# Chained PSUM sums for the gate and up projections, and the norm's second product moved to the gate's side

## The chip, the cores and the metric

The kernel runs on one core of a Trainium2 chip. The metric is the device time of one execution in microseconds (us). TensorE is called PE in the profile (PEld is its weight load), VectorE DVE, ScalarE ACT, GpSimd POOL, SyncE SP; a q behind an engine's name means its sequencer.

## What is computed

The reference is one step of a streaming encoder with one layer: attention with two groups of heads, an output projection with a residual, then a SwiGLU feed-forward block with a residual, and a last norm. There are 16 meta tokens, 512 of a prompt and 64 of a sample; the 576 of prompt and sample go through the feed-forward block. The change touches only the second half of a layer:

```python
x = x + mix @ lp['w_out']
h = rmsnorm(x, lp['norm_ffn_g'])
x = x + (jax.nn.silu(h @ lp['ffn_w_gate']) * (h @ lp['ffn_w_up'])) @ lp['ffn_w_down']
```

D_MODEL is 2048 and D_FF 5632; everything is float32.

## The kernel before

**Precision.** A float32 product is made of three matmuls. Each operand is split into a high part (rounded to the matmul's type, written by ACT, L156) and a low part (the difference, written by DVE, L153), and high x high, high x low and low x high are added in PSUM. Weights are split when they have been loaded: the tiles `wh` and `wl`, two buffers each. The tokens' operands are split once for a stage: `bh` and `bl`.

**Seven products for eight.** Gate, up and down multiply two by two blocks of 128 x 128 weights with two by two blocks of 128 x 288 tokens by Winograd's form of Strassen's scheme. `winograd` (L993) runs the seven products. Products 1, 2 and 4 take a block of the raw weights (a11, a12, a22) as it is; 5 and 7 take a sum and a difference that POOL makes (`subtotal`, L1013, called by `lhs`); 6 is made by DVE from 5's, and 3 by DVE from 6's. The sums lie in `ws`, three buffers. For each product, the matmuls with `wh` run over all slots (L1051: `bh` and `bl`), then those with `wl` (L1055). Then `take` adds the product to what the call makes, and `step` runs a piece of other work that is threaded in.

**Order and banks.** `ORDER` (L937) is 1, 2, 4, 5, 6, 3, 7, each product in a PSUM bank of its own. The down projection gives `chain=CHAIN` instead (L1263): 1, 5, 6, 2, 7, 3, 4, in three banks. Products 1, 6, 7 and 4 share bank "a", 5 and 3 bank "b", and 2 has "c". What lies in a shared bank is a running sum, which `take` reads at points on the way; a matmul into a shared bank has to wait until the last reading of it is done.

**Gate and up.** The loop over u (L1185, 22 times) makes 256 columns of gate, then of up: one `winograd` call each, with eight slots of 256 rows of the model dimension, so 7 x 24 matmuls. A call loads two raw tiles of 1 MB, one for each half of the slots (L1193). There are three buffers for them, one in pool `rw` and two in `fr`, so that one half of the next call can be loaded a call ahead, and the other goes where the first half of the present call lay. The result goes to a tile `c` of two rows f of 576 tokens, as four quarters c11, c12 (row 0) and c21, c22 (row 1): one buffer for the gate (tag `cg`), two for up (`cu`). `combined` (L1118) makes the take: an ACT copy of product 1 into a tile `s` (L1125) and seven DVE sums (L1128 to L1137). For c11 that is L1137, after product 2, the second of the call.

**After a pair of calls** (L1214): for each row f, DVE multiplies g by the token norm `rb2` (L1215), ACT takes the Silu (L1216), POOL multiplies w (up's result) by `rb2` (L1217) and by g (L1218), and the row is stored to DRAM. For u below 20, POOL then makes four sums of w's quarters (L1224 to L1227) in a view `t` of the gate's tile, and SP stores them (`sumspill`). Only when that store has read them may the next gate call write its tile.

**Down.** The results are brought back as operands by `builder` (L1141), in blocks of 4 slots or, for the last block, 2. Its first block is built during the last up call, by product in `ORDER` (L1153, `by_product`).

**What sets the order.** In these stages a scheduler that builds the program lays out each engine's instructions by when it expects them to be ready; the text's order is the priority. Only down's builder pins some. Loads and stores are issued by SP.

Of the kernel before, what the change touches and what calls it, by code (L numbers as in the profile page):

```python
# [13 lines left out]
AF = mybir.ActivationFunctionType  # L14
ALU = mybir.AluOpType
# [100 lines left out]
def encoder_step(  # L116
# [8 lines left out]
    V, S, G = nc.vector, nc.scalar, nc.gpsimd  # L125
# [10 lines left out]
    def load(dst, src):  # L136
        nc.sync.dma_start(dst, src)
# [11 lines left out]
    def f32(ap):  # L149
        return ap.bitcast(F32)  # L150
# [44 lines left out]
    def project(ps, wsrc, xs, dup=False):  # L195
        for hf in range(2):
            wh, wl = weights(
                wsrc[hf * 8 * P:(hf + 1) * 8 * P, :].rearrange("(k p) c -> p k c", p=P), 8, P, dup)
            for k in range(8):
                kc = hf * 8 + k  # L200
                mm3([ps[:, 0, 0:TH], ps[:, 1, 0:TH]], wh[:, k, :], wl[:, k, :],
                    halves(xs[kc][0]), halves(xs[kc][1]), kc == 0, kc == KC - 1)
                yield 0
# [110 lines left out]
    with ExitStack() as ph:  # L314
# [30 lines left out]
        with tc.tile_pool(name="xn", bufs=1) as xn:  # L345
# [59 lines left out]
            first = project(ps0, w_in[:, 0:P], xs1)  # L405
# [24 lines left out]
        for j, (o, n) in enumerate(tok):  # L430
            b = o // TH
# [194 lines left out]
    with ExitStack() as ph:  # L626
# [288 lines left out]
        first = st.spawn(0, latents())  # L915
# [12 lines left out]
    def pool(name, side="left"):  # L928
        cm = tc.tile_pool(name=name, bufs=1, side=side)
        return cm.__enter__(), lambda: cm.__exit__(None, None, None)  # L930
# [3 lines left out]
    rb2 = rw.tile([P, TQ], F32, name="rb2")  # L934
    sq2 = rw.tile([P, TQ], F32, name="sq2")
    operands = {}
    ORDER = (1, 2, 4, 5, 6, 3, 7)  # L937

    def pin(ins):
        if pinned[0]:  # L940
            tc.keep_in_program_order(ins)
# [3 lines left out]
    def operand(m, p, src):  # L945
        hi = bc.tile([P, QH], F32R, name=f"bh{p}_{m}")
        lo = bc.tile([P, QH], F32R, name=f"bl{p}_{m}")
        pin(S.activation(hi, src, AF.Copy))
        pin(V.tensor_tensor(lo, src, f32(hi), op=ALU.subtract))
        operands[m, p] = (hi, lo)  # L950

    def quarters(b1, b2):
        return b1[:, 0:QH], b1[:, QH:TQ], b2[:, 0:QH], b2[:, QH:TQ]

    def token_operands(pool, m, b1, b2):

        b11, b12, b21, b22 = quarters(b1, b2)

        def sum_tile():
            return pool.tile([P, QH], F32, name="bs", tag="bs", bufs=2)  # L960

        operand(m, 1, b11)
        yield
        operand(m, 2, b21)
        yield
        t = sum_tile()
        pin(G.tensor_tensor(t, b12, b11, op=ALU.subtract))
        operand(m, 5, t)
        yield
        pin(G.tensor_tensor(t, b22, t, op=ALU.subtract))  # L970
        operand(m, 6, t)
        yield
        pin(G.tensor_tensor(t, t, b21, op=ALU.subtract))
        operand(m, 4, t)
        yield
        operand(m, 3, b22)
        yield
        t = sum_tile()
        pin(G.tensor_tensor(t, b22, b12, op=ALU.subtract))
        operand(m, 7, t)  # L980
        yield

    def load_raw(pool, src, r0, nk, c0, bufs, tag="raw"):
        r = pool.tile([P, nk, 256], F32, name="raw", tag=tag, bufs=bufs)
        load(r, src[r0:r0 + nk * P, c0:c0 + 256].rearrange("(k p) c -> p k c", p=P))
        return r
# [121 lines left out]
    fw, close_fw = pool("fw")  # L1108
# [3 lines left out]
    fb, close_fb = pool("fb", "right")  # L1112


    def stile():
        return fr.tile([P, QH], F32, name="s", tag="s", bufs=4)

    def combined(c11, c12, c21, c22):  # L1118

        s = {}  # L1120

        def take(p, banks):
            if p == 1:
                s[1] = stile()
                S.activation(s[1], banks[1], AF.Copy)  # L1125
            elif p == 6:
                s[2] = stile()
                V.tensor_tensor(s[2], s[1], banks[6], op=ALU.add)  # L1128
                V.tensor_tensor(c12, s[2], banks[5], op=ALU.add)
            elif p == 3:  # L1130
                V.tensor_tensor(c12, c12, banks[3], op=ALU.add)
            elif p == 7:
                V.tensor_tensor(s[2], s[2], banks[7], op=ALU.add)
                V.tensor_tensor(c22, s[2], banks[5], op=ALU.add)
                V.tensor_tensor(c21, s[2], banks[4], op=ALU.subtract)
            elif p == 2:
                V.tensor_tensor(c11, s[1], banks[2], op=ALU.add)  # L1137

        return take

    def builder(m0, count, plain, ahead, by_product=False):  # L1141

        srcs = {}
        for m in range(m0, m0 + count):
            quarter = [actspill[2 * m + f, :, c] for f in range(2) for c in (slice(0, QH), slice(QH, TQ))]
            if plain:
                for p, src in zip((1, 2, 4, 5), quarter):
                    srcs[m, p] = src
            else:
                for p, src in zip(ORDER, (quarter[0], quarter[2], sumspill[m, :, 2], sumspill[m, :, 0],  # L1150
                                          sumspill[m, :, 1], quarter[3], sumspill[m, :, 3])):
                    srcs[m, p] = src
        todo = sorted(srcs, key=lambda mp: ORDER.index(mp[1])) if by_product else list(srcs)  # L1153

        def fetch(n):
            for m, p in todo[n:n + 1]:
                hi = bc.tile([P, QH], F32R, name=f"bh{p}_{m % 8}")
                lo = bc.tile([P, QH], F32R, name=f"bl{p}_{m % 8}")
                load(f32(lo), srcs[m, p])
                operands[m % 8, p] = (hi, lo)  # L1160

        for n in range(ahead):
            fetch(n)
        for n, (m, p) in enumerate(todo):
            fetch(n + ahead)
            hi, lo = operands[m % 8, p]
            pin(S.activation(hi, f32(lo), AF.Copy))
            yield
            pin(V.tensor_tensor(lo, f32(lo), f32(hi), op=ALU.subtract))
            yield  # L1170

    def token_norm():
# [4 lines left out]
        rsqrt(rb2, sq2)  # L1177
        yield

    blocks = [4, 4, 4, 4, 4, 2]  # L1180

    turn = 0
# [2 lines left out]
    for u in range(FC // 2):  # L1185
        out = {}
        for which, wsrc in (("g", w_gate), ("u", w_up)):
            first = turn == 0
            raws = []
            for hf in range(2):  # L1190
                if turn:
                    rp, bufs = (rw, 1) if turn % 3 == 0 else (fr, 2)
                    raws.append(load_raw(rp, wsrc, hf * 1024, 8, u * 256, bufs))  # L1193
                turn += 1
            c = fb.tile([P, 2, TQ], F32, name="c", tag="cg" if which == "g" else "cu", bufs=1 if which == "g" else 2)
            take = combined(*quarters(c[:, 0, :], c[:, 1, :]))
            done = [0]

            def step():
                if u == 0 and which == "u":  # L1200
                    next(norm, None)
                if u == FC // 2 - 1 and which == "u":
                    done[0] += 1
                    if done[0] > 2:
                        for _ in range(2 * blocks[0]):
                            next(start, None)

            if first:
                winograd(fw, fb, raws, range(4, 8), take, banks0, step=step)
            else:  # L1210
                winograd(fw, fb, raws, range(8), take, step=step)
            out[which] = c
        g, w = out["g"], out["u"]
        for f in range(2):  # L1214
            V.tensor_tensor(g[:, f, :], g[:, f, :], rb2, op=ALU.mult)  # L1215
            S.activation(g[:, f, :], g[:, f, :], AF.Silu)  # L1216
            G.tensor_tensor(w[:, f, :], w[:, f, :], rb2, op=ALU.mult)  # L1217
            G.tensor_tensor(w[:, f, :], w[:, f, :], g[:, f, :], op=ALU.mult)  # L1218
            if u < FC // 2 - 1:
                store(actspill[2 * u + f], w[:, f, :])  # L1220
        if u < FC // 2 - blocks[-1]:
            b11, b12, b21, b22 = quarters(w[:, 0, :], w[:, 1, :])
            t = g.rearrange("p f (h c) -> p (f h) c", h=2)
            G.tensor_tensor(t[:, 0, :], b12, b11, op=ALU.subtract)  # L1224
            G.tensor_tensor(t[:, 1, :], b22, t[:, 0, :], op=ALU.subtract)
            G.tensor_tensor(t[:, 2, :], b21, t[:, 1, :], op=ALU.subtract)
            G.tensor_tensor(t[:, 3, :], b22, b12, op=ALU.subtract)  # L1227
            store(sumspill[u], t)
# [12 lines left out]
    def plain_rows(m0, n, d, hs, slots, done):  # L1241
# [13 lines left out]
        for f in range(2):  # L1255
            for h in hs:
                c = y[2 * d + f][:, h * QH:(h + 1) * QH]
                V.tensor_tensor(c, c, banks[f, h], op=ALU.add)  # L1258
                done(2 * d + f, h)

    CHAIN = ((1, "a"), (5, "b"), (6, "a"), (2, "c"), (7, "a"), (3, "b"), (4, "a"))  # L1263

    def down_rows(m0, n, d, slots, step):
        raws = [load_raw(fr, w_down, m0 * 256, 2 * n, d * 256, 2)]
# [6 lines left out]

        winograd(yp, yp, raws, slots, take, step=step, chain=CHAIN)

# [42 lines left out]
    first = 0  # L1318
# [100 lines left out]
```

## Time and profile before

| | before |
|---|---|
| median of 3 runs | 2583.15 us (2583.13 to 2589.03) |
| the profiled execution | 2593.06 us |
| its span, first to last instruction | 2590.9 us |
| mean granted TensorE clock | 0.983 |
| gate and up, about | 1000 to 2010 us |
| of it 20 blocks u, 1054.5 to 1963.5 | 909 us |

The profile is of one execution. Its rows give the start, the length, the engine, the line and the operation with out<-in, and in brackets the idle time of that engine just before and what ended it. A matmul's row is some 0.29 us long, but a new one starts every 0.13 us. In a view of waits the columns are the total, the number and the longest. In a view of stretches each engine has its busy time and number of instructions, and behind them stand the granted TensorE clock, the busy share of the DMA engines and GB/s.

### The profile page before, as it was taken

What the parts mean: (1) busy time and instruction counts of PE and PEld (TensorE: products, weight loads), DVE (VectorE), ACT (ScalarE), POOL (GpSimd) and SP (SyncE); (2) the same over time, 40 slices, a digit from 0 to 9 for tenths busy, and PEclk for the clock granted to TensorE, in tenths of its full rate; (3) what the DMA queues carried; (4) which work ended last, traced back from release to release, by engine and by line L of the source; (5) the groups of instructions that cost most, each with busy time, mean ns of one, the idle gap of its engine ahead of it and who ended that gap; (6) DMA issues with size and microseconds to landing.
All of it is one profiled execution on the core that took longest, in us unless ns stands there. A gap on an engine that the chain in (4) does not pass through costs nothing. (4 is left out here: it accounts for less than half of the span.)

```text
span 2590.9 us, 44881 instructions
## 1 busy us (share of the span) xinstructions
PE 2464.9 (95%) x17847; PEld 2399.3 (93%) x17847; DVE 1837.4 (71%) x2955; ACT 1056.5 (41%) x1879; POOL 763.5 (29%) x614
## 2 busy tenths in 40 slices
PE   6999999989999999999999999999999899999997
PEld 5999999988999888999999999999999899999996
DVE  5455555556565568777677787777778899899874
ACT  5234333334443444333333333333334344444444
POOL 0000000000000265545545455464543221221244
PEclk9999999999999899999999999999999899999998
DMA  6433233334331553333333333333335543443334
GB/s 197 126 93 93 80 86 86 81 104 121 99 99 58 170 152 124 106 113 121 130 116 108 111 122 128 116 128 108 109 126 177 189 146 98 146 146 101 98 107 130
DMA packets 330563, 307.73 MB, mean 119 GB/s; under 512 B 24707, under 2 KB 298506, under 8 KB 330354
## 3 DMA queue, kind: packets, MB, share of 16 engines
q1 hardware_dynamic: 330354, 304.87, 37.7%
q8 instruction: 140, 2.29, 0.4%
q14 instruction: 69, 0.57, 0.1%
HBM read 250.82 MB, written 56.68 MB: 119 GB/s over the span
## 5 line engine op out<-in xcount | busy, mean ns | idle before, releaser
L1051 PE MATMUL m<-bh,wh 128*128 128x288 f32 x3584 | 971.8, 296 | 8.3 <-ACT wh L156 6.3
L1051 PE MATMUL m<-bl,wh 128*128 128x288 f32 x3584 | 970.4, 295 | 0.0
L1051 PEld LDWEIGHTS m<-bh,wh 128*128 128x128 f32 x3584 | 676.3, 189 | 10.7 <-ACT wh L156 8.2
L1051 PEld LDWEIGHTS m<-bl,wh 128*128 128x128 f32 x3584 | 680.0, 190 | 0.1
L1055 PE MATMUL m<-bh,wl 128*128 128x288 f32 x3584 | 589.3, 300 | 38.1 <-DVE wl L153 35.9
L1020 POOL TENSOR_TENSOR ws<-raw 128x512 f32<-128x512 f32 x256 | 359.3, 1412 | 765.1 <-DVE wl L153 533.6
L1055 PEld LDWEIGHTS m<-bh,wl 128*128 128x128 f32 x3584 | 512.2, 189 | 57.1 <-DVE wl L153 56.4
L156 ACT ACTIVATE wh<-ws 128x512 fp32r<-128x512 f32 (+1 forms) x340 | 288.3, 848 | 475.9 <-PE m L1051 339.2
L153 DVE TENSOR_TENSOR wl<-ws,wh 128x512 fp32r<-128x512 f32 (+1 forms) x340 | 377.5, 1115 | 56.7 <-ACT wh L156 52.7
L153 DVE TENSOR_TENSOR wl<-raw,wh 128x512 fp32r<-128x512 f32 x416 | 401.2, 985 | 14.3 <-ACT wh L156 14.1
L156 ACT ACTIVATE wh<-raw 128x512 fp32r<-128x512 f32 x416 | 248.0, 625 | 339.6 <-PE m L1051 297.6
L108 PE MATMUL ps<-xh,wh 128*128 128x296 f32 x992 | 228.9, 312 | 6.9 <-ACT wh L156 6.9
L108 PE MATMUL ps<-xl,wh 128*128 128x296 f32 x992 | 218.3, 302 | 0.0
L108 PE MATMUL ps<-xh,wl 128*128 128x296 f32 x992 | 218.1, 301 | 0.0
L108 PEld LDWEIGHTS ps<-xh,wh 128*128 128x128 f32 x992 | 163.1, 192 | 11.1 <-ACT wh L156 7.0
L108 PEld LDWEIGHTS ps<-xl,wh 128*128 128x128 f32 x992 | 163.5, 191 | 0.0
L108 PEld LDWEIGHTS ps<-xh,wl 128*128 128x128 f32 x992 | 163.1, 191 | 0.3 <-DVE wl L153 0.3
L1020 DVE TENSOR_TENSOR ws<-ws,raw 128x512 f32<-128x512 f32 x128 | 94.0, 737 | 97.6 <-POOL ws L1020 92.5
L153 DVE TENSOR_TENSOR wl<-wr,wh 128x1024 fp32r<-128x1024 f32 (+1 forms) x110 | 117.7, 1070 | 45.3 <-ACT wh L156 36.4
L1272 DVE TENSOR_TENSOR y<-y,m 128x288 f32<-128x288 f32 x280 | 125.4, 448 | 21.5 <-PE m L1055 20.3
L156 ACT ACTIVATE wh<-wr 128x1024 fp32r<-128x1024 f32 (+1 forms) x110 | 101.8, 929 | 80.5 <-PE ps L108 72.2
L518 POOL MEMSET bias<- 64x64 f32 x8 | 1.4, 170 | 409.7 <-DMA bias<-tsk 247.8
(361 smaller groups left out, 3426.7 us busy)
## 6 DMA issues: line engine op xcount, KB each, us to landing
raw<-in_ffn_w_gate SPq DMA_DIRECT2D x44, 1024.0 KB, 7.7
raw<-in_ffn_w_up SPq DMA_DIRECT2D x44, 1024.0 KB, 6.3
raw<-in_ffn_w_down SPq DMA_DIRECT2D x40, 1024.0 KB, 5.4
wr<-in_w_in SPq DMA_DIRECT2D x60, 512.0 KB, 4.0
actspill<-c SPq DMA_DIRECT2D x44, 288.0 KB, 2.2
sumspill<-c SPq DMA_DIRECT2D x20, 576.0 KB, 3.0
bl<-sumspill SPq DMA_DIRECT2D x80, 144.0 KB, 3.4
bl<-actspill SPq DMA_DIRECT2D x68, 144.0 KB, 4.1
```

Source lines behind the costliest of these rows:

```text
L108: self.tc.keep_in_program_order(self.pe.matmul(out, lhsT, rhs, start=start, stop=stop))
L153: V.tensor_tensor(lo, src, f32(hi), op=ALU.subtract)
L156: S.activation(hi, src, AF.Copy)
L518: G.memset(bias[0:64, 464:528], -BIG)
L1020: engine.tensor_tensor(w[:, k:k + m, :], pick(xs), pick(ys), op=op)
L1051: PE.matmul(banks[p], wh[:, k, :], x, start=first and new and k == 0 and x is hi, stop=False, skip_group_check=not new)
L1055: PE.matmul(banks[p], wl[:, k, :], hi, start=False, stop=last and k == n - 1, skip_group_check=not new)
L1272: V.tensor_tensor(c, c, banks[p], op=ALU.add)
```

## The change

The calls of gate and up, all but the first gate call (whose first half is done earlier, with banks of its own), run in `CHAIN`'s order with its three banks. `combined` gets a second take for them: products 1, 5, 6 and 4 are copied from their bank by ACT into c11, c22, c12 and c21, and products 2, 7 and 3 are added by DVE to c11, c22 and c12. For the running sum in bank "a" to come out, product 4 has to be added where it was subtracted, so its token operand changes sign: in `token_operands` the operands of a difference are swapped (L973), and the old take adds it (L1135). The builder of the first down block goes by `CHAIN`'s order too.

The gate's side now does its norm and Silu in `gated`: DVE times `rb2`, Silu, and POOL times `rb2` a second time. That is done right after the gate's call, for the first u after up's. Up's result is then multiplied by g alone. `CHAIN` moves to the top.

```diff
+    CHAIN = ((1, "a"), (5, "b"), (6, "a"), (2, "c"), (7, "a"), (3, "b"), (4, "a"))
...
-        pin(G.tensor_tensor(t, t, b21, op=ALU.subtract))
+        pin(G.tensor_tensor(t, b21, t, op=ALU.subtract))
         operand(m, 4, t)
...
-    def combined(c11, c12, c21, c22):
+    def combined(c11, c12, c21, c22, chained):
 
         s = {}
+        copied, added = {1: c11, 5: c22, 6: c12, 4: c21}, {2: c11, 7: c22, 3: c12}
+
+        def take_sums(p, banks):
+            if p in copied:
+                S.activation(copied[p], banks[p], AF.Copy)
+            else:
+                V.tensor_tensor(added[p], added[p], banks[p], op=ALU.add)
+
+        if chained:
+            return take_sums
...
-                V.tensor_tensor(c21, s[2], banks[4], op=ALU.subtract)
+                V.tensor_tensor(c21, s[2], banks[4], op=ALU.add)
...
-        todo = sorted(srcs, key=lambda mp: ORDER.index(mp[1])) if by_product else list(srcs)
+        order = [p for p, _ in CHAIN]
+        todo = sorted(srcs, key=lambda mp: order.index(mp[1])) if by_product else list(srcs)
...
+    def gated(g):
+
+        for f in range(2):
+            V.tensor_tensor(g[:, f, :], g[:, f, :], rb2, op=ALU.mult)
+            S.activation(g[:, f, :], g[:, f, :], AF.Silu)
+            G.tensor_tensor(g[:, f, :], g[:, f, :], rb2, op=ALU.mult)
...
-            take = combined(*quarters(c[:, 0, :], c[:, 1, :]))
+            take = combined(*quarters(c[:, 0, :], c[:, 1, :]), not first)
...
-                winograd(fw, fb, raws, range(8), take, step=step)
+                winograd(fw, fb, raws, range(8), take, step=step, chain=CHAIN)
             out[which] = c
+            if u and which == "g":
+                gated(c)
         g, w = out["g"], out["u"]
+        if u == 0:
+            gated(g)
         for f in range(2):
-            V.tensor_tensor(g[:, f, :], g[:, f, :], rb2, op=ALU.mult)
-            S.activation(g[:, f, :], g[:, f, :], AF.Silu)
-            G.tensor_tensor(w[:, f, :], w[:, f, :], rb2, op=ALU.mult)
             G.tensor_tensor(w[:, f, :], w[:, f, :], g[:, f, :], op=ALU.mult)
```

More of the change, by code (lines that the diff above doesn't have):

```diff
@@ L1259, in plain_rows @@
                 done(2 * d + f, h)
-    CHAIN = ((1, "a"), (5, "b"), (6, "a"), (2, "c"), (7, "a"), (3, "b"), (4, "a"))
     def down_rows(m0, n, d, slots, step):
```

## The prediction

> **What bounds the kernel now.** I read the page first: the busy shares, then the slices.
>
> ```profile
> span 2590.9 us, 44881 instructions
> ...
> PE 2464.9 (95%) x17847; PEld 2399.3 (93%) x17847; DVE 1837.4 (71%) x2955; ACT 1056.5 (41%) x1879; POOL 763.5 (29%) x614
> ...
> PE   6999999989999999999999999999999899999997
> ...
> PEclk9999999999999899999999999999999899999998
> ```
>
> TensorE is busy nearly throughout. Gate and up run from about 1000 to 2010 us, slices 15 to 31. The dip at slice 31 is the passage into the down projection. The view by stretches over 20 steady blocks, and the waits over the same stretch, say how much is left to gain there:
>
> ```profile
> 1054.50:1963.50 909.00, 892.81 (x6655) 887.37 (x6654) 694.90 (x878) 340.94 (x478) 459.95 (x315) 1.00 0.36 118
> ```
> ```profile
> PE m L1055 <- DVE wl L153: 16.2, 21, 1.9
> ```
>
> The columns of the first row are length, then PE, PEld, DVE, ACT and POOL busy. A block u (one gate call and one up call) takes 909/20 = 45.45 us. DVE is at 76%, ACT at 38%. The only wait of TensorE's matmuls in the stretch is 16.2 us, for the low half of a weight split. One block shows the beat and the place of that wait; below are the third pass of each product on PE, then the wait behind it on DVE:
>
> ```profile
> 1405.87 1.24 PE L1055 MATMUL m<-bh,wl 128*128 128x288 f32 x8
> ...
> 1409.06 1.24 PE L1055 MATMUL m<-bh,wl 128*128 128x288 f32 x8
> ...
> 1412.25 1.24 PE L1055 MATMUL m<-bh,wl 128*128 128x288 f32 x8
> ...
> 1425.72 1.33 PE L1055 MATMUL m<-bh,wl 128*128 128x288 f32 x8 [0.53 <-DVE wl L153]
> ```
> ```profile
> 1417.73 1.82 DVE L153 TENSOR_TENSOR wl<-ws,wh 128x1024 fp32r<-128x1024 f32 x1
> 1424.07 0.46 DVE L1137 TENSOR_TENSOR c<-s,m 128x288 f32<-128x288 f32 x1 [4.52 <-DMA sumspill<-c]
> 1424.44 2.35 DVE L153 TENSOR_TENSOR wl<-ws,wh 128x1024 fp32r<-128x1024 f32 x2
> ```
>
> A product takes 3.19 us (1409.06 less 1405.87), 133 ns for each of its 24 matmuls. The up call ends with the row of 1409.06, at 1410.30; the next gate's products then begin at 1410.1, 1413.3, 1416.5 and so on. L1137 writes c11 after the gate's second product. The gate has one tile `c`, and block u's sums of quarters lie in it until their store has landed. So DVE waits 4.52 us in front of it, the splits behind it are late, and PE loses 0.53 us here, 16.2 us in all. The chain behind that wait, on POOL and on SP:
>
> ```profile
> 1408.60 1.82 POOL L1217 TENSOR_TENSOR c<-c,rb 128x576 f32<-128x576 f32 x1 [4.24 <-DVE c L1131]
> 1410.49 1.76 POOL L1218 TENSOR_TENSOR c<-c 128x576 f32<-128x576 f32 x1
> 1412.33 1.15 POOL L1224 TENSOR_TENSOR c<-c 128x288 f32<-128x288 f32 x1
> 1413.61 1.81 POOL L1217 TENSOR_TENSOR c<-c,rb 128x576 f32<-128x576 f32 x1
> 1415.50 1.76 POOL L1218 TENSOR_TENSOR c<-c 128x576 f32<-128x576 f32 x1
> 1417.34 1.14 POOL L1225 TENSOR_TENSOR c<-c 128x288 f32<-128x288 f32 x1
> 1418.43 1.79 POOL L1227 TENSOR_TENSOR c<-c 128x288 f32<-128x288 f32 x1
> 1420.18 0.81 POOL L1226 TENSOR_TENSOR c<-c 128x288 f32<-128x288 f32 x1
> ```
> ```profile
> 1421.02 0.32 SPq L140 DMA_DIRECT2D sumspill<-c  x1
> ```
>
> The store is issued at 1421.02 and DVE goes on at 1424.07: 3.05 us.
>
> **Part one: the takes.** A chained call has 4 ACT copies and 3 DVE adds where there were 1 and 7. That holds for 43 of the 44 calls (the first gate call keeps its form).
>
> ```profile
> L1125 ACT ACTIVATE s<-m x44: 387/402/417, 1005.2 to 1984.1; 128x288 f32<-128x288 f32 x44
> ```
> ```profile
> L1135 DVE TENSOR_TENSOR c<-s,m x41: 435/442/450, 1068.2 to 1983.0; 128x288 f32<-128x288 f32 x41
> ```
>
> DVE loses 43 x 4 x 0.442 = 76 us, ACT gains 43 x 3 x 0.402 = 52 us. Neither sets the pace (76% and 38% above), so I count both at nothing beyond the wait that falls away: L1137 no longer stands, waiting, ahead of the splits on DVE. That returns at most the 16.2 us, which I take whole: **-16**. The swapped operands at L973 cost nothing: same instruction, same sizes.
>
> **Part two: the gate's tile is wanted earlier.** This is the term that decides. In the new order the first product's bank is copied by ACT into c11, one product sooner than L1137: after product one, at 1413.4. The third product (number 6) adds into the same bank, so it may not begin, at 1416.5, before that copy is done. When is the tile free? The second step of the change shortens the tail: L1217 leaves the up side. From the POOL rows, in the clock of this block:
>
> - row f=0 is ready with the take of product 3, about 1407.7 (its matmuls end at 1407.1); L1218 to 1409.5, L1224 to 1410.6;
> - row f=1 is ready after product 4, now last: ACT's copy of c21 (0.40 us) ends at about 1410.9; L1218 to 1412.6, L1225 to 1413.8, L1227 and L1226 to 1416.4;
> - 3.05 us for the store: 1419.5, against 1424.07 now, 4.6 us sooner; the copy to 1419.9.
>
> That is 3.4 us after the third product is due. A subtotal for the next call's product 5 (1.3 us, the rows of 1400.04 and 1402.83 below) can fall between on POOL, since it is now needed one product after the call begins: 4.7 us. From below: the scheduler that builds the order of each engine may put product 2, which has a bank of its own, into the gap, wholly (0 us) or in part. The present order shows how far it misjudges this: it has put L1137 between two splits that DVE could otherwise have run without idling, and 4.52 us are lost in front of it. A plan that wrong by that much will fill only a part. Ends 0 and 4.7; I take **3.0 us** for each of the 20 gate calls behind a sums store: **+60**. Behind the waiting copy on ACT stand the splits for the following products; they come late by the same amount and not more, since product 6 runs 3.19 us after it.
>
> **Clock.** A stall of TensorE can cost more than its length. Three places:
>
> ```profile
> 996.04 0.40 PE L1051 MATMUL m<-bh,wh 128*128 128x288 f32 x1 [1.83 <-ACT wh L156]
> ...
> 2006.03 0.61 PE L1051 MATMUL m<-bh,wh 128*128 128x288 f32 x1 [2.81 <-ACT wh L156]
> ```
> ```profile
> 996.00:1000.00 4.00, 3.96 (x28) 1.00 0.08 25
> ...
> 2024.00:2029.50 5.50, 5.49 (x22) 0.50 0.43 164
> ...
> 2002.00:2030.00 28.00, 17.32 (x71) 0.57 0.65 208
> ```
>
> (The columns are length, PE busy and count, granted clock.) After 1.83 us idle the clock stayed at 1.00; after 2.81 us it was 0.50, and from the last idle there the half clock lasted some 5.5 us, with 22 matmuls where 41 would fit: 2.5 us lost. My stall of 3.0 lies at that edge; ends 0 and 20 x 2.5 = 50 us, taken for 8 of the 20: **+20**. [...]
>
> **Part three: raw weights are held longer.** Now the last reader of a raw tile is the subtotal for product 7, long before the call ends:
>
> ```profile
> 1396.34 2.54 POOL L1020 TENSOR_TENSOR ws<-raw 128x512 f32<-128x512 f32 x2 [12.00 <-DVE wl L153]
> 1400.04 1.29 POOL L1020 TENSOR_TENSOR ws<-raw 128x512 f32<-128x512 f32 x1 [1.16 <-DVE wl L153]
> 1402.83 1.52 POOL L1020 TENSOR_TENSOR ws<-raw 128x512 f32<-128x512 f32 x1 [1.50 <-DMA raw<-in_ffn_w_gate]
> ```
> ```profile
> 1397.66 0.37 SPq L137 DMA_DIRECT2D raw<-in_ffn_w_gate  x1
> 1398.91 0.37 SPq L137 DMA_DIRECT2D raw<-in_ffn_w_up  x1
> ```
>
> The gate's second raw half is issued at 1397.66 and read at 1402.83, 5.2 us later, 7.3 us before its call starts. In the new order the last reader is the split for product 4, the last product. That split waits for the weight buffer of the fifth product, so it runs about two products before the end: DVE is through with the first half at about 1404.6 (1410.1 less 6.4, plus a split of some 0.7). The half lands at 1404.7 + 5.2 = 1409.9, in time by a few tenths: the next call's first product needs it split about 1 us after 1410.1. Ends 0 and 1 us for each of 43 calls; also the Silu now stands at the gate-to-up seam, where ACT may wait for DVE's product in front of it. Both together at 0.1 us a call: **+4**.
>
> **Part four: into the down projection.** In the 28 us of the last row above, 71 matmuls would need 71 x 0.133 = 9.4 us: 18.6 us are lost while the operands of the first down block are built in the order 1,2,4,5,6,3,7 and wanted in 1,5,6,2,7,3,4. After the change both orders agree, and the last up call frees the operand buffers in that order too. Ends 0 (DVE, which makes them all, stays as loaded) and 18.6; less than half of it: **-8**.
>
> **The sum:** -16 + 60 + 20 + 4 - 8 = +60 us. The profiled execution took 2593.06 us with its span of 2590.9; the median of the runs is 2583.15, 9.9 lower, so I set the change on the median: 2583 + 60 = **2643 us**.
>
> **Rivals.**
>
> *The tile is free in time (faster).* If the scheduler's order puts product 2 ahead of product 6 for the whole gap, the 60 and 20 vanish and -16 + 4 - 8 = -20 remain: 2563. For it: L1217's removal takes 4.6 us off the tail, and L1224 of f=0 standing ahead of L1217 of f=1 shows that the order follows readiness, not the text. Against: the 4.52 us in front of L1137.
>
> *A small stall that gives the gain back (same).* About 1 us a block: 20 + 4 - 24 = 0: 2583.
>
> *Raw halves late as well (slower still).* If the DMA takes 1 us longer than 5.2, each call waits 1 us: 43 more, 2686. For it: a slack of tenths; against: 5.2 us was measured with a second megabyte issued 1.25 us behind it.
>
> *Half clock at each stall.* With 4 us stalls and all 20 gated: -16 + 80 + 50 + 4 - 8 = +110: 2693.
>
> *The takes were never the bound.* Then the 76 us of DVE bring nothing, which the sum already supposes.
>
> **How the numbers follow.** Forecast (a stall of 2 to 4 us a block, 2600 to 2680): 0.47. Free in time: 0.27. Give and take: 0.07. Raw late: 0.10. Half clock throughout: 0.09. What a measurement can tell from no change is 0.3%, 8 us. Faster 0.27, same 0.07, slower 0.66. The range goes from 2558, a little under the faster rival, to 2705, past the half clock; it leaves out under 2 in 10. The forecast's own range is 2600 to 2680.
>
> **What would show it.** Right: a wait of ACT's copy into `c` for the sums store, about 20 times and 5 us or more each; a wait of PE for that copy at the third product of each gate call, 2 to 4 us; granted clock below 1.00 in slices 15 to 31; a block of 48 to 50 us in place of 45.45. Wrong: a block of 44.7 us (14 x 3.19) and no such PE wait, or PE waiting at a call's first product for raw weights instead. The passage near 2002 to 2030 should be shorter by some 8 us, with operands ready in the order used.

## The result, and the profile after

| | before | after |
|---|---|---|
| median of 4 runs each | 2583.14 us | 2718.89 us (2714.83 to 2723.0) |
| ratio | | 1.0518, 95% interval 1.0503 to 1.0532 |
| the profiled execution | 2593.06 us | 2714.83 us |
| its span | 2590.9 us | 2713.1 us |
| mean granted TensorE clock | 0.983 | 0.978 |

The change costs 136 us where 60 were forecast, and 2719 lies above the range (2558 to 2705). By the profiled executions it is 122 us of span: the one of before was 9.9 us above its median, the one of after 4.1 below.

First the page of after, the same lines as before's:

```profile
span 2713.1 us, 44758 instructions
...
PE 2493.0 (92%) x17847; PEld 2415.7 (89%) x17847; DVE 1840.4 (68%) x2783; ACT 1106.3 (41%) x2008; POOL 766.5 (28%) x614
...
PE   6999999989999998888989888998988899999996
...
PEclk8999999989998999999999999999999999999998
```

Of the 17 nines of gate and up (slices 15 to 31, counted from 0) 12 have become eights, while the clock's digits there are nines as before. DVE, relieved of 172 instructions (2955 less 2783), has the same busy time as before, in a longer span. Now the view by stretches. A whole number of blocks is cut out by the store of a block's first result row: from that of u = 0 to that of u = 20 it is 20 blocks. First the kernel before, then the kernel after, then one block of the latter from 1460.42:

```profile
1043.43:1960.07 916.64, 900.26 (x6710) 894.58 (x6709) 698.74 (x881) 342.87 (x478) 468.65 (x320) 1.00 0.36 118
```
```profile
1039.76:2090.87 1051.11, 934.98 (x6714) 914.50 (x6713) 701.75 (x720) 390.26 (x600) 472.89 (x320) 0.98 0.31 104
...
1460.42:1512.79 52.37, 47.46 (x338) 46.34 (x337) 35.05 (x36) 19.61 (x31) 22.57 (x17) 0.97 0.31 104
```

A block takes 52.6 us on average where it took 45.8 (the 909 us named ahead of the result are a little less than 20 blocks, so 45.45 is a little low); 20 of them are 134.5 us longer. PE idles 1051.1 - 935.0 = 116.1 us of it, against 916.6 - 900.3 = 16.4, and its busy time has grown by 34.7. The view of PE's waits over the same stretch gives the idle time its names:

```profile
PE m L1058 <- DVE wl L153: 45.6, 20, 2.5
PE m L1054 <- ACT wh L156: 38.3, 39, 2.2
PE m L1054 <- ACT c L1128: 32.1, 20, 2.4
```

The three make 116.0 us, all of it. Only the last, 32.1 us, is the wait that the prediction is built on (the gate's tile). The first two, 83.9 us, are waits for split weights. The block from 1460.42, by the timeline of each engine (start, length, instruction, idle time before), shows where those come from:

```profile
1454.61 1.29 DVE L153 TENSOR_TENSOR wl<-raw,wh 128x512 fp32r<-128x512 f32 x2
...
1455.35 0.37 SPq L137 DMA_DIRECT2D raw<-in_ffn_w_gate  x1
...
1460.47 0.63 ACT L156 ACTIVATE wh<-raw 128x512 fp32r<-128x512 f32 x1 [3.48 <-DMA raw<-in_ffn_w_gate]
...
1460.62 2.54 POOL L1023 TENSOR_TENSOR ws<-raw 128x512 f32<-128x512 f32 x2
...
1461.94 1.76 DVE L1023 TENSOR_TENSOR ws<-ws,raw 128x512 f32<-128x512 f32 x1 [3.46 <-POOL ws L1023]
...
1462.54 0.70 PE L1058 MATMUL m<-bh,wl 128*128 128x288 f32 x4
...
1463.12 1.84 POOL L1240 TENSOR_TENSOR c<-c 128x576 f32<-128x576 f32 x1
...
1463.63 1.88 DVE L153 TENSOR_TENSOR wl<-raw,wh 128x512 fp32r<-128x512 f32 x1
...
1465.57 1.18 PE L1058 MATMUL m<-bh,wl 128*128 128x288 f32 x4 [2.32 <-DVE wl L153]
...
1472.04 0.71 ACT L1128 ACTIVATE c<-m 128x288 f32<-128x288 f32 x2 [0.83 <-DMA sumspill<-c]
...
1472.50 0.40 PE L1054 MATMUL m<-bh,wh 128*128 128x288 f32 x1 [0.90 <-ACT c L1128]
...
1482.21 1.28 DVE L153 TENSOR_TENSOR wl<-raw,wh 128x512 fp32r<-128x512 f32 x2
...
1487.61 1.43 POOL L1199 TENSOR_TENSOR c<-c,rb 128x576 f32<-128x576 f32 x1 [6.00 <-issue]
...
1493.68 1.91 DVE L1023 TENSOR_TENSOR ws<-ws,raw 128x512 f32<-128x512 f32 x1
...
1496.73 0.40 PE L1054 MATMUL m<-bh,wh 128*128 128x288 f32 x1 [1.59 <-ACT wh L156]
1496.97 0.29 PE L1054 MATMUL m<-bl,wh 128*128 128x288 f32 x1
```

Read it from the top. The first of the two splits at 1454.61, those for product 4, ends near 1455.3, and with it the raw tile it reads comes free: the gate's second raw half is issued at 1455.35, 5.1 us before its call begins at 1460.42, and ACT splits it at 1460.47. So the half arrives at the beginning of the call, as computed, and ACT has the high part ready at 1461.10. But then three instructions want that half at once: the split's low part (DVE), POOL's sum for product 5, and DVE's subtraction for product 6, which needs POOL's sum. The program has laid that subtraction ahead of the low part on DVE. DVE stands 3.46 us for POOL, subtracts from 1461.94 to 1463.70, and splits only then, until 1465.5. PE, which had done the first four matmuls with `wl` at 1462.54, idles 2.32 us. DVE's two instructions are slow besides: 1.76 and 1.88 us with POOL at work, where the same split takes 0.64 at 1482.21 (two in 1.28), in the 6.00 us before 1487.61 that POOL stands idle. At 1496.73, in the up call, PE waits again, for the split of product 6's operand, the end of the same chain: POOL's sum, DVE's subtraction (1493.68), ACT's split. There the product with the norm that the change has put at this place stands ahead of the subtraction on DVE too (L1197, 1490.77, 1.85 us).

At the end of the stage the first sum of the down projection (`y`) comes 132.3 us later than before, the last 122.0 (before: 2023.5 and 2496.8), by the view of that line:

```profile
L1290 DVE TENSOR_TENSOR y<-y,m x280: 439/448/456, 2155.8 to 2618.8; 128x288 f32<-128x288 f32 x140
```

Down gives 10.3 us back.

### The profile page after: what moved, and what is told of

It reads as the page before. It is cut to its first block, busy times and chain, and to the rows that moved or that the text cites. A ratio compares the mean times of both kernels' runs of the same rounds, so it can differ in the third digit from the quotient of the medians.

```text
span 2713.1 us, 44758 instructions
## 1 busy us (share of the span) xinstructions
PE 2493.0 (92%) x17847; PEld 2415.7 (89%) x17847; DVE 1840.4 (68%) x2783; ACT 1106.3 (41%) x2008; POOL 766.5 (28%) x614
## 5 line engine op out<-in xcount | busy, mean ns | idle before, releaser
L1054 PE MATMUL m<-bh,wh 128*128 128x288 f32 x3584 | 989.3, 301 | 78.1 <-ACT wh L156 43.9
L1054 PE MATMUL m<-bl,wh 128*128 128x288 f32 x3584 | 981.2, 298 | 0.0
L1054 PEld LDWEIGHTS m<-bh,wh 128*128 128x128 f32 x3584 | 685.1, 191 | 94.5 <-ACT wh L156 55.3
L1054 PEld LDWEIGHTS m<-bl,wh 128*128 128x128 f32 x3584 | 688.3, 192 | 0.1
L1058 PE MATMUL m<-bh,wl 128*128 128x288 f32 x3584 | 595.6, 301 | 62.3 <-DVE wl L153 60.7
L153 DVE TENSOR_TENSOR wl<-raw,wh 128x512 fp32r<-128x512 f32 x416 | 382.7, 937 | 64.6 <-ACT wh L156 58.6
L1023 DVE TENSOR_TENSOR ws<-ws,raw 128x512 f32<-128x512 f32 x128 | 139.6, 1091 | 87.1 <-POOL ws L1023 79.8
L1130 DVE TENSOR_TENSOR c<-c,m 128x288 f32<-128x288 f32 x129 | 58.6, 454 | 163.2 <-PE m L1058 163.2
```

The source lines that it names most:

```text
L1023: engine.tensor_tensor(w[:, k:k + m, :], pick(xs), pick(ys), op=op)
L1054: PE.matmul(banks[p], wh[:, k, :], x, start=first and new and k == 0 and x is hi, stop=False, skip_group_check=not new)
L1058: PE.matmul(banks[p], wl[:, k, :], hi, start=False, stop=last and k == n - 1, skip_group_check=not new)
L1130: V.tensor_tensor(added[p], added[p], banks[p], op=ALU.add)
```

## The experiments

The theory after the result: two causes, raw halves that come too late for a chain of engines behind them, and the gate's single tile; they hide one another. The rivals: the tile alone, the raw halves alone, the move of the norm, or the order of instructions on DVE. Each run was compared with the kernel before on the same chip, so the ratios are what to compare; where a difference of two ratios is put in us below, it holds within some 9 us.

**One cause at a time.** A second buffer for the gate's tile:

```diff
-            c = fb.tile([P, 2, TQ], F32, name="c", tag="cg" if which == "g" else "cu", bufs=1 if which == "g" else 2)
+            c = fb.tile([P, 2, TQ], F32, name="c", tag="cg" if which == "g" else "cu", bufs=2)
```

> The changed kernel with a second buffer for the gate's tile, so that no copy waits for the sums store. If the tile was the main loss (the forecast's part two), the 20 stalls behind it and their half clock go: about 2719 - 100 = 2620. If the late raw weights are the main loss, only the 32 us of PE waits for the copy and a part of the half clock go: 2670 to 2690, and the waits for weight splits (45 and 36 us) stay.

Measured: 2691.52 us, ratio 1.0395 [1.0365, 1.0425]. PE's waits, 1050 to 2080 us:

```profile
PE m L1058 <- DVE wl L153: 46.8, 20, 2.5
PE m L1054 <- ACT wh L156: 35.9, 39, 1.6
```

The wait for the tile is gone, the others stand as they were. That is just above the 2670 to 2690 expected if the raw weights are the main loss. The ratio fell by 0.0123, 32 us: the tile's own price in this kernel, what its row said. The raw halves are the larger part.

A fourth raw buffer, paid for with two of the small tiles `s`, so that both halves can be loaded a call ahead:

```diff
-                    rp, bufs = (rw, 1) if turn % 3 == 0 else (fr, 2)
+                    rp, bufs = {0: (rw, 1), 3: (fw, 1)}.get(turn % 4, (fr, 2))
```

> The changed kernel with a fourth raw buffer, so that both halves of a call's weights are loaded well ahead (two of the four small tiles s are given up for the room). If the late raw weights are the main loss: the 81 us of PE waits for weight splits nearly vanish, and 2600 to 2640 comes out, with the wait for the gate's tile still there at 2 to 4 us a block. If the tile is the main loss: above 2690.

Measured: 2678.78 us, 1.0346 [1.0316, 1.0376], above what was expected. PE's waits (1050 to 2050), the stretch of 19 blocks from the first store of the sums to the last, then one block on SP, ACT and PE:

```profile
PE m L1054 <- ACT c L1128: 71.1, 20, 5.5
```
```profile
1052.46:2015.12 962.66, 897.14 (x6384) 892.63 (x6384) 656.61 (x685) 367.55 (x570) 463.68 (x305) 0.94 0.33 107
```
```profile
1458.65 0.34 SPq L140 DMA_DIRECT2D sumspill<-c  x1
...
1461.53 0.71 ACT L1128 ACTIVATE c<-m 128x288 f32<-128x288 f32 x2 [3.35 <-DMA sumspill<-c]
...
1461.99 0.61 PE L1054 MATMUL m<-bh,wh 128*128 128x288 f32 x1 [3.40 <-ACT c L1128]
```

Every wait for weights has gone, 84 us of them, but the time falls by only 0.0172 x 2589 = 45. The tile's wait has grown to 71.1, 3.6 us a block. That is the other face of the finding: while PE came late by 2.3 us at the gate's first product, the store of the sums had 2.3 us more to land, and the wait for it looked small. The stall is 3.40 us in the block shown, and the granted clock over the 19 blocks is 0.94 where it was 0.98.

**Both together.** The fourth raw buffer, and products 1 and 5 copied into small tiles of their own, so that bank and tile are no longer tied:

```diff
-            if p in copied:
+            if p in (1, 5):
+                s[p] = stile()
+                S.activation(s[p], banks[p], AF.Copy)
+            elif p in copied:
                 S.activation(copied[p], banks[p], AF.Copy)
             else:
-                V.tensor_tensor(added[p], added[p], banks[p], op=ALU.add)
+                V.tensor_tensor(added[p], {2: s.get(1), 7: s.get(5)}.get(p, added[p]), banks[p], op=ALU.add)
```

> The changed kernel with a fourth raw buffer and with the copies of products 1 and 5 in small tiles of their own, so that neither the raw weights nor the gate's tile can be late. If the two together are the whole loss, though each alone gave back only 27 and 40 of some 130 us: no PE waits in gate and up, and 2555 to 2575, below the kernel before by the recovered 16 us and some 10 us at the passage to down. If the shared banks or the new order cost something by themselves: 2600 or more.

Measured: 2558.5 us, 0.9896 [0.9867, 0.9925], as expected. The view by stretches:

```profile
1300.00:1500.00 200.00, 200.00 (x1505) 200.00 (x1504) 157.38 (x160) 86.65 (x134) 113.15 (x74) 1.00 0.38 125
```

PE is busy for 200.00 of 200 us, at the full clock. So the two causes, with what they do to the clock, are the whole loss: with both away, the change's order, its chained sums and its move of the norm are 0.0104 x 2589 = 27 us faster than before (19 to 34 by the interval). Taken singly, curing the tile or the raw halves brought 32 and 45 of the 161 us (1.0518 - 0.9896, of 2589) that lie between.

**The order without the shared banks.** The new order, each product in a bank of its own, with the old take:

```diff
-                winograd(fw, fb, raws, range(8), take, step=step, chain=CHAIN)
+                winograd(fw, fb, raws, range(8), take, step=step, chain=[(p, p) for p, _ in CHAIN])
```

> The changed kernel's order of products alone: each product has a bank of its own and the old take with seven DVE sums, so no matmul waits for a reading of its bank. Late raw weights: they are as late as in the changed kernel, so the waits for weight splits stay and 2670 to 2710 comes out. If sharing the banks was the loss: near the time before, 2580 to 2600.

Measured: 2643.93 us, 1.0211 [1.0182, 1.0241], lower than expected. PE's waits, 1050 to 2050:

```profile
PE m L1054 <- ACT wh L156: 39.8, 28, 1.7
PE m L1058 <- DVE wl L153: 14.0, 20, 0.8
```

The order alone costs 0.0211 x 2589 = 55 us, and the two waits for weights make 53.8 of it. The tile costs nothing here: the old take first writes it after product 6, the third, where the changed kernel copies into it after the first, and no bank is shared; no wait for the store of the sums shows up on any engine. Shared banks with the early copies add the rest, by the difference to the changed kernel.

**The order of instructions on DVE.** In the block above, the subtraction for product 6 stood ahead of the split's low part. Here it is held behind the splits written before it:

```diff
-                engine.tensor_tensor(w[:, k:k + m, :], pick(xs), pick(ys), op=op)
+                ins = engine.tensor_tensor(w[:, k:k + m, :], pick(xs), pick(ys), op=op)
+                if hold:
+                    tc.keep_in_program_order(ins)
...
-                s = sums[2] = subtotal(n, engine, ALU.subtract, [sums[1]], a11)
+                s = sums[2] = subtotal(n, engine, ALU.subtract, [sums[1]], a11, bool(chain) and n == 8)
```

> The changed kernel with DVE's subtraction for product 6 (L1023) held behind the splits traced before it. The raw half still lands when it does. If the loss at a gate's first product comes from DVE's queue (the low half of its split stands behind that subtraction, which waits for POOL), the 45 us of PE waits for DVE's split vanish or halve, and the wait for the copy into the gate's tile grows in their place: 2670 to 2715. If it comes from the landing alone, nothing changes: 2710 to 2725.

Measured: 2771.38 us, 1.0719 [1.0686, 1.0753]: slower than the change itself. The waits of PE and of ACT, 1050 to 2050, and the stretch of 19 blocks:

```profile
PE m L1056 <- ACT wh L156: 88.8, 53, 2.4
...
PE m L1056 <- ACT c L1130: 26.9, 18, 1.9
...
ACT wh L156 <- DVE ws L1023: 148.3, 36, 4.4
```
```profile
1044.27:2095.45 1051.18, 928.89 (x6384) 909.15 (x6384) 710.72 (x685) 368.38 (x571) 466.27 (x305) 0.93 0.30 98
```

PE no longer waits for DVE's splits at all. The stall has moved down the chain: ACT waits 148.3 us for DVE's subtractions, and PE for ACT. This order of the queue moved the lateness and did not remove it. But it isn't the waits that make the run slower: a block is 55.3 us in place of 52.6, of which PE idles 6.4 in place of 5.8. The other 2.1 us are busy time, with the clock at 0.93 against 0.98. The expectation was wrong in its sign.

**The old order with the change's sums.** Order 1, 2, 4, 5, 6, 3, 7 in four banks, takes by copy and add as in the change, the norm on the gate's side, and only the last up call in the new order:

```diff
+    SUMS = ((1, "a"), (2, "c"), (4, "d"), (5, "b"), (6, "a"), (3, "b"), (7, "a"))
...
+        copied = {1: c11, 4: c21, 5: c22, 6: c12}
+        added = {2: (c11,), 7: (c22,) if late else (c22, c21), 3: (c12,)}
...
-                winograd(fw, fb, raws, range(8), take, step=step, chain=CHAIN)
+                winograd(fw, fb, raws, range(8), take, step=step, chain=CHAIN if late else SUMS)
```

> Running sums in PSUM in the old order 1,2,4,5,6,3,7 with four banks (4 copies on ACT, 4 sums on DVE); only the last up call has the new order. Raw tiles come free as early as before, and product 6, which needs the first bank read, is the fifth. Late raw weights as the cause: no PE waits for raw, 2565 to 2590. If sharing banks or the copy into the gate's tile costs by itself: 2610 or more.

Measured: 2559.81 us, 0.9886 [0.9858, 0.9915], a little below what was expected. The same kernel once more:

> Running sums in the old order with four banks once more, for an interval: PE has almost no waits in gate and up, and the passage to down is shorter. A ratio of 0.986 to 0.991 to the kernel before.

Measured: 2565.97 us, 0.9898 [0.9883, 0.9913], as expected. Two views of the first of these, stretches and the waits of ACT:

```profile
1300.00:1500.00 200.00, 200.00 (x1505) 200.00 (x1505) 150.28 (x170) 85.85 (x133) 102.29 (x74) 1.00 0.37 124
```
```profile
ACT c L1130 <- DMA sumspill<-c: 60.7, 20, 4.8
```

ACT's copy still waits for the store of the sums, up to 4.8 us, in every block. But the next product into that bank, 6, is the fifth here and not the third, and PE doesn't notice. So the wait itself costs nothing here; in the changed kernel its place two products ahead of PE does. This version is 1.0% faster than the kernel before, and by the ratios the changed kernel takes 1.0518 / 0.9898 = 1.063 times as long.

**An order that frees the raw tiles earlier.** That version again, with its takes and four banks, but the products in the order 1, 5, 6, 2, 4, 7, 3, and the gate's tile doubled as in the first run:

```diff
-    SUMS = ((1, "a"), (2, "c"), (4, "d"), (5, "b"), (6, "a"), (3, "b"), (7, "a"))
+    SUMS = ((1, "a"), (5, "b"), (6, "a"), (2, "c"), (4, "d"), (7, "a"), (3, "b"))
...
-            c = fb.tile([P, 2, TQ], F32, name="c", tag="cg" if which == "g" else "cu", bufs=1 if which == "g" else 2)
+            c = fb.tile([P, 2, TQ], F32, name="c", tag="cg" if which == "g" else "cu", bufs=2)
```

> Order 1,5,6,2,4,7,3: product 4, whose split is the last reader of the raw weights, is the fifth product instead of the last and has a bank of its own; the gate's tile has two buffers, and there are three raw buffers as in the changed kernel. If it is the raw tile held to the last product that makes the next half late, the raw half comes two products (6.4 us) sooner, no PE waits remain, and 2555 to 2580 comes out, against 2692 with the second tile buffer alone. If the early need of products 5 and 6 is enough to stall PE: 2620 or more.

Measured: 2594.9 us, 1.0014 [1.0002, 1.0026], some 15 us over what was expected, but 0.038 below the first run (1.0395). Against that one, product 4 stands fifth and not last, and has a bank of its own. PE's waits, 1050 to 2000:

```profile
PE m L1056 <- ACT c L1130: 7.5, 21, 0.4
PE m L1060 <- DVE wl L153: 7.3, 32, 0.6
```

The 2.5 us waits for weights are gone; many of a few tenths remain. They make 14.8 us, about half of the 30 by which this version lies above the one before; where the rest goes the waits don't show. With product 4 last, its split is the last reader of the raw half; with it in fifth place that reader comes two products earlier. That speaks for the late release as the root of the loss, though the fourth bank changed with it; the fourth raw buffer above changed the loads alone.

**The move of the norm.** First the change with the second product back on up's side, as the kernel before has it:

```diff
-            if u and which == "g":
-                gated(c)
...
-        if u == 0:
-            gated(g)
         for f in range(2):
+            V.tensor_tensor(g[:, f, :], g[:, f, :], rb2, op=ALU.mult)
+            S.activation(g[:, f, :], g[:, f, :], AF.Silu)
+            G.tensor_tensor(w[:, f, :], w[:, f, :], rb2, op=ALU.mult)
             G.tensor_tensor(w[:, f, :], w[:, f, :], g[:, f, :], op=ALU.mult)
```

> The changed kernel with the norm's second product back on up's side, so that the tail on POOL has two more products of 1.8 us, one of them on the path to the sums store. Theory: the store lands some 2 to 4 us later and PE waits for the gate's tile that much longer, 20 times: 2760 to 2800. If the tail is hidden behind the late raw weights: within 15 us of the changed kernel.

Measured: 2799.39 us, 1.0828 [1.0786, 1.0869], as expected. PE's waits, 1050 to 2050:

```profile
PE m L1058 <- DVE wl L153: 83.3, 35, 3.8
PE m L1054 <- ACT c L1128: 58.8, 18, 4.8
```

Then the kernel before with the move alone:

> The kernel before with the norm's second product moved to the gate's side alone. The tail on POOL is shorter, the sums store lands earlier, and DVE's wait of 4.5 us in front of L1137 shrinks: the 16 us of PE waits fall to 0 to 8, so 2573 to 2586 where the kernel before takes 2589.

Measured: 2598.54 us, 1.0028 [1.0018, 1.0038]; a small gain had been expected. The waits of PE, DVE and ACT, 1050 to 2000:

```profile
PE m L1055 <- DVE wl L153: 14.5, 36, 1.0
...
DVE c L1137 <- DMA sumspill<-c: 77.9, 20, 4.6
...
ACT c L1184 <- DVE c L1183: 138.4, 42, 5.0
```

In the new kernel the move saves 0.031, 80 us: it takes POOL's work off the tail in front of the store and off the first products of the gate call, and without it PE's waits for the tile and for the low halves are both larger than in the changed kernel. The clock is lower without it too (0.963 and 0.956 over the two runs, 0.975 to 0.978 with it). In the old kernel the tail gets shorter as well (L1137 waits 77.9 us where it waited 92.3), and the Silu, now at the seam of gate and up, makes ACT wait 138.4 us for DVE's product, where it waited 66.1 (at L1216). PE's own waits hardly change, 14.5 us against 16.2. The kernel is 0.3% slower all the same, and these waits don't show why: 19 blocks take 882.7 us in place of 871.2, and it is PE's busy time that has grown, by 12.0 us at a clock of 1.00.

**The passage into down alone.** The kernel before, with the new order for the last up call and for the builder of the first down block:

```diff
-        todo = sorted(srcs, key=lambda mp: ORDER.index(mp[1])) if by_product else list(srcs)
+        order = [p for p, _ in CHAIN]
+        todo = sorted(srcs, key=lambda mp: order.index(mp[1])) if by_product else list(srcs)
...
-                winograd(fw, fb, raws, range(8), take, step=step)
+                winograd(fw, fb, raws, range(8), take, step=step, chain=[(p, p) for p, _ in CHAIN] if late else ())
```

> The kernel before with only the last up call in the order 1,5,6,2,7,3,4 (banks of its own) and the first down block's operands built in that order. Theory: the passage into down shortens by the 10 us that the changed kernel's down part gained: 8 to 14 us under the kernel before. If that gain came from elsewhere: no difference.

Measured: 2584.06 us, 0.9978 [0.9967, 0.999], less than expected. The passage in the view by stretches, of this kernel and then of the kernel before:

```profile
2000.00:2032.00 32.00, 24.70 (x139) 23.44 (x139) 25.78 (x44) 11.12 (x23) 10.67 (x7) 0.79 0.75 250
```
```profile
2000.00:2032.00 32.00, 21.32 (x100) 19.59 (x100) 25.81 (x41) 11.02 (x27) 11.52 (x8) 0.63 0.63 200
```

39 more matmuls in the same 32 us, at 0.133 us each 5.2 us; by the ratio 5.7 (2.6 to 8.5). In the two profiles the first sum `y` of down comes 9.1 us sooner (2014.4 for 2023.5), the last 7.1. DVE is as busy as before (25.8), and it makes the operands.

## Why the prediction was wrong

The sign and the mechanism of its main term were right; the time missed, since one small term was priced by the wrong event. That the sign was right was not luck: with the raw halves cured and the tile alone left the ratio is 1.0346, 90 us, where the prediction's sum without part three is 56. Term by term, over the 20 blocks, measured as after less before:

| term | predicted | measured |
|---|---|---|
| part one, DVE's wait in the takes | -16 | -16.4 (PE's waits of before, all counted as gone) |
| part two, the gate's tile | +60 | +32.1 |
| part three, raw weights held longer | +4 | +83.9 |
| clock | +20 | about +17 |
| matmul time beyond the clock | 0 | about +18 |
| sum of the blocks | +68 | +134.5 |
| part four, into down | -8 | see below |

**The step that failed: part three.** "The half lands at 1404.7 + 5.2 = 1409.9, in time by a few tenths ... Ends 0 and 1 us for each of 43 calls ... Both together at 0.1 us a call: +4." The half's arrival was right to a few tenths: issued 5.1 us ahead of its call, read by ACT 0.05 us after the call's start. What was priced is only whether the first reader, ACT's split, is in time. In the new order product 5 comes second and product 6 third, so the chain behind that half (POOL's sum, DVE's subtraction, ACT's split) is wanted within two products, 6.4 us. Before, products 2 and 4 stood between, each with raw weights as they are. The price was 83.9 / 40 = 2.1 us a call and not 0.1, and its upper end of 1 us was too low as well. The rival "raw halves late as well", with 43 us, named the right waits at half the size, but for a cause that was not there: a DMA slower than 5.2 us, where the half took 5.1. (The prediction's own terms put the release of the raw tile at 1404.4, where it writes 1404.6 and 1404.7; that changes nothing.) The experiments carry this: the fourth buffer takes these waits away entirely, and the order alone, without the shared banks, costs 55 us through them.

**Part two: right mechanism, hidden size.** 3.0 us a block were predicted. The changed kernel shows 32.1 / 20 = 1.6, as its PE arrives late already. With the raw halves cured it is 71.1 / 20 = 3.6, inside the ends of 0 and 4.7 and near the value taken. The prediction added its terms as if they were independent; a lateness ahead of a wait is subtracted from it. The sign "about 20 times and 5 us or more each" for the copy's wait did not come true: it is 31.6 us in all, and with the raw halves cured still 70.1, 3.5 us each. The tail did get shorter, but by less than the 4.6 us predicted. From the first matmul of the gate's call to the issue of the store of the sums it is 10.9 us before (1410.13 to 1421.02), 8.7 in the changed kernel (1460.42 to 1469.15) and 7.1 with the raw halves cured (1451.51 to 1458.65). In the changed kernel two of POOL's subtotals stand in that tail (1460.62, 2.54 us), where the upper end allowed for one. That the move is needed is shown (80 us without it).

**Clock.** In 12 of the 21 gate calls with a stall for DVE's split the clock is lower behind it, in 9 it stays at 1.00. Taken block by block, PE is busy for 47.4 us where it fell and 45.9 where it held, so 1.5 us each, 17 for the 11 such blocks of the 20. The sum has the size forecast, but not by its way: the stalls are 2.3 to 2.5 us, not 3.0. Nor is it a cost of its own here. The wait for the tile that follows is 0.85 to 1.35 us where the clock fell and 2.4 us where it held, and the beat is the same: in four blocks in a row PE goes on at 1106.13, 1158.33, 1210.53 and 1262.73, every 52.2 us, after waits of 0.86, 0.85, 2.44 and 2.44 us. What the half clock took, the tile's wait gave back: one more lateness that hides another. With the raw halves cured, at a clock of 0.94, PE's busy time is 44 us longer over 20 blocks than before, so in the kernel that the prediction had in mind the 20 us were too few. The other 18 us by which PE's busy time grew in the changed kernel are settled in part. The first matmul after the wait at 1496.73 has a row of 0.40 us for 0.29, as those at 1472.50 and 1524.86 have, and keeps the next one off for 0.24 in place of 0.13 (until 1496.97); at 0.11 us for each of the 79 waits of the 20 blocks that would be 9.

**Parts one and four.** The sum of their gains, -24, is what the kernel with both causes cured has: -27 by its ratio, -19 to -34 by the interval. For part four by itself, 5.7 us were measured where 8 were taken, which the interval (2.6 to 8.5) still holds. Down is 10.3 us shorter in the profile of after, but two profiles of one and the same kernel (the old order with the change's sums) have 471.3 and 475.7 us for it, so a good part of that is not the change's.

**The range** missed by 14 us. One rival did join the two causes, the forecast's 60 with 43 for the raw halves, 2686; none joined them at the size that the raw halves had, and the half clock throughout was counted with the tile alone. With 84 us in place of 4, the prediction's sum reads 2723, near the 2719 measured. That is in part luck, since the tile's row came out 28 us lower than taken and the matmul time 18 us higher.

## What to carry to other kernels

When a reordering makes a buffer free later, price the load not by whether it lands before its first reader, but by the whole chain of engines behind it, up to the last product that is now wanted early, with each engine's queue as it stands. Two latenesses in one block hide one another: cure one and the other can grow, as the tile's wait did here from 32 to 71 us, so that neither single cure tells what both are worth (32 and 45 us of 161 here). Order and accumulation can be separated: the sums in PSUM with the old order kept the gain (0.9898) without the loss.

## What the runs showed of the hardware

The clock did not follow the length of a stall alone. In the changed kernel a wait of 2.32 us for the same instruction stands in two neighbouring blocks. The views by stretches over the 3.61 us behind it, and the next wait of PE in the second block (in the first it is the row of 1472.50 above, with 0.90 us), read:

```profile
1465.57:1469.18 3.61, 3.61 (x15) 3.61 (x16) 3.58 (x3) 1.06 (x1) 3.55 (x3) 0.53 0.22 82
1517.94:1521.55 3.61, 3.61 (x27) 3.61 (x28) 3.58 (x3) 1.73 (x3) 3.57 (x3) 1.00 0.22 82
```
```profile
1524.86 0.40 PE L1054 MATMUL m<-bh,wh 128*128 128x288 f32 x1 [2.41 <-ACT c L1128]
```

Half the clock, 15 matmuls, in the one; the full clock and 27 in the other. Why one and not the other was not found. Of the 20 stalls of 2.3 to 2.5 us for that split, 12 had a lower clock over the 3.61 us behind them (0.53 to 0.68), and 8 had 1.00.

A DVE subtraction of two 128x512 operands took 0.64 us with POOL idle (1482.21) and 1.88 us with POOL at work (1463.63). The prediction had put the split at 0.7. Not every split with POOL at work was slow: at 1457.80 one took 0.69 us, though POOL's product of 1457.96 (L1240, 1.81 us) ran beside most of it. No run kept POOL away from the slow split alone, so how much of the 2.32 us stall goes back to POOL stays open.
